# Order of weight loads, of the mixing's loads, and of transposes and fetches in the last gate of a two-layer Fox/RWKV and gMLP block

## The chip, the core and the metric

The kernel runs on one core of one Trainium2 chip. The metric is the device time of one execution in microseconds. The kernel before took 2281.07 us (median of three runs, 2279.98 to 2284.08).

## What is computed

A block of two layers on x (512 rows, 2048 columns), all in fp32. For each layer i:

```
h = h + rms_norm(y, norm_post[i])                       # y: the layer's own branch
h = h + (p[i] @ ple_w_proj[i]) * sigmoid(h @ ple_w_gate[i])
```

In layer 0, y comes from a forgetting attention and an RWKV time mix. In layer 1 it comes from a gated mixing of chunks of 128 rows:

```
u, v, g = split(rms_norm(h) @ c_w_in)                   # 3 x 2048 columns
v = layer_norm(gelu(v), c_ln_g, c_ln_b)
mixed[g] = tril(c_w_s[g]) @ v[chunk, group g] + c_b_s[g] # 16 groups of 128 columns
y = (gelu(u) * mixed * silu(g)) @ c_w_out
```

## The kernel before

TensorE (PE) gets fp32 accuracy by splitting each operand in a high and a low part, so that each product takes three matmuls. The weights' high part `whi` is a cast on ACT (L1387 in layer 1), the low part `wlo` a subtraction on DVE (L1388). There are four buffers of each, so these casts can run at most four pieces ahead of PE.

**The products of seven.** The products with `c_w_in` and with the last `ple_w_gate` are made by a scheme that needs seven block products instead of eight (`seven`, L1393 on). A *step* is one block product: eight *pieces* of W (128 x 512 each), with six matmuls per piece, so 48 matmuls. Layer 1's `c_w_in` takes 42 steps (called 0 to 41 below), the last gate in `last_layer` 14 more (42 to 55). I number the pieces of the last gate 0 to 111: step 42 is pieces 0 to 7, step 43 pieces 8 to 15, step 46 pieces 32 to 39, step 51 pieces 72 to 79.

**Where a piece of W comes from.** `pieces` (L1327) makes each pair of pieces from a tile of 128 x 1024. `load` brings it by a 512 KB DMA on SP's queue (L1338, tiles `raw` and `rq`). For some block products it is a sum of two blocks: `grow` adds the second block by an accumulating DMA on POOL's queue (L1342); `add` adds a tile that was loaded on its own (L1346, on DVE); and the product numbered 4 adds two 256 KB `half` tiles, loaded by SP (L1380, one buffer for each of two names), on DVE.

**What sets the order.** A tile scheduler puts each engine's instructions in order by priority and by when it expects their inputs. Each engine, SP and the DMA-issuing part of ACT included, then works strictly in that order: an instruction that waits holds up all behind it. The casts and the adds of W carry a raised priority (`wpri`, 150000 at this point); the loads of W do not. Side work is hung on a counter: `tick` counts pieces, and `later(n, step)` runs `step` n pieces on.

**The mixing.** `mix(g)` (L1491) is called for 16 groups during steps 21 to 27 and 35 to 41. Its four parts lie 11 and 4 pieces ahead of, at, and 5 pieces after a given piece: `load` brings the group's v (`vn<-vd`), `ws`, `ln_g` and `ln_b` by four DMAs on ACT's queue (L1502 to L1505), the last three into slices of one tile (`rstdB` or `accq`); `norm` normalises v with four ACT instructions (L1511) and multiplies and adds by the rows on DVE (L1515, L1516); `split` makes high and low parts (L1526, L1527); `mul` is the product (L1531 to L1533).

**The last gate.** `last_layer` (L1108) has side work in its 14 steps. `flip(g, m)` transposes a block of h on PE into one PSUM bank (four 128 x 128 matmuls, L1164), copies it out on ACT (L1166, into `xl`, or into the scratch tiles `sq` and `sg` for m = 2 and 3) and stores it to DRAM (`rd`, L1167). There are eight banks named `mm`, which the products share. `late(q)`, `s24(q)`, `s3(q)` and `x22` update h and make the other operands of the scheme, mostly on DVE. `fetch` loads the pieces of `pd` and `rd` that a result needs, 256 KB each, on SP (L1208, L1209), into tiles named `yh` at first and later into slices of two `xh` tiles that become free when `x22` has read them. `emit` makes the result (L1212 to L1215) and stores it (L1217).

The first layer's gate (`dense_all`, L970 on, with the loads and casts of L169 to L181) runs before layer 1: SP loads `raw` (L169), ACT and DVE split it (L179, L181), and the first loads of `c_w_in` for layer 1 are issued during it.

## Time and profile before

| | |
|---|---|
| median of three runs | 2281.07 us |
| profiled execution | 2283.18 us |
| its span on the core | 2281.5 us (1.7 us lie around it) |
| mean granted TensorE clock | 0.992 |
| instructions | 39072 |
| DMA traffic | 311.59 MB, mean 137 GB/s |
| first layer's gate | about 1190 to 1386 us |
| layer 1, steps 0 to 41 | up to 1874 us |
| last gate, steps 42 to 55 | 2086.15 to 2273.34 us |

The profiled execution lies 2.11 us (0.09%) above the median. A busy share is a mean over the whole span; the short waits in the stages that the change touches are read from the timelines and windows of those stages. A number in square brackets in a timeline is the time that the engine was idle just before, with what ended it.

### The profile page before, as it was taken

To read this page: it belongs to the slowest core of one execution; us is meant where nothing else is said; L and a number is where in the kernel's file an instruction comes from. 1 tells how busy PE (TensorE), PEld (TensorE's weight loads), DVE (VectorE), ACT (ScalarE), POOL (GpSimd) and SP (SyncE) were. 2 spreads that over 40 slices of the span, in tenths; PEclk is the share of its full clock that TensorE was granted. 3 is DMA by queue.
4 is the path that set the end of the run, shared out by engine and by line. 5 is a ranking of instruction groups with operands and counts; after the bars stand their busy time and mean duration, and the time that the engine had idled before them with its cause. 6 is when DMAs were issued, how large, how long until landed. Compare 5 with 4: busy or idle time off the path is not lost.

```text
span 2281.5 us, 39072 instructions
## 1 busy us (share of the span) xinstructions
PE 2228.9 (98%) x14787; PEld 1822.5 (80%) x14787; DVE 1476.4 (65%) x2885; ACT 1226.8 (54%) x2510; POOL 244.2 (11%) x302
## 2 busy tenths in 40 slices
PE   8999999999999999999999999999999999999988
PEld 7878888888887888878888888878778778887766
DVE  8666667666643878872237448778688684227867
ACT  5455555555443777753244547546566654335644
POOL 2000010010100000000010112101111110010020
PEclk9999999999999999999999999999999999999999
DMA  6322232223234533343335446776767774337696
GB/s 232 91 78 71 71 86 81 73 67 84 75 97 132 163 102 98 101 148 98 97 102 168 130 122 162 194 204 165 196 179 186 217 205 133 101 102 213 197 253 186
DMA packets 299482, 311.59 MB, mean 137 GB/s; under 512 B 15213, under 2 KB 198670, under 8 KB 298270
## 3 DMA queue, kind: packets, MB, share of 16 engines
q1 hardware_dynamic: 255390, 253.52, 36.6%
q0 software_dynamic: 17408, 33.56, 8.6%
q10 hardware_dynamic: 26496, 22.03, 3.1%
q8 instruction: 116, 1.90, 0.3%
q14 instruction: 72, 0.59, 0.1%
HBM read 274.15 MB, written 34.90 MB: 135 GB/s over the span
## 4 chain that ended last, share of the span: by engine, by line
PE 82%; DVE 7%; DMA 6%; ACT 3%; issue 2%; SPq 0%; ACTq 0%; DVEq 0%; POOLq 0%
PE mm L195 11%; PE mm L197 11%; PE mm L196 11%; PE mm L982 6%; PE mm L983 6%; PE mm L981 6%; PE mm L1415 6%; PE mm L1416 6%; PE mm L1417 6%; DVE wlo L1388 2%; PE tm L533 1%; DMA sq<-vd 1%; DVE rq L1346 1%; PE tm L554 1%; DMA rq<-in_ple_w_gate_dram 1%
## 5 line engine op out<-in xcount | busy, mean ns | idle before, releaser
L181 DVE TENSOR_TENSOR wlo<-raw,whi 128x512 fp32r<-128x512 f32 x464 | 331.6, 722 | 423.5 <-ACT whi L179 382.8
L179 ACT CAST whi<-raw 128x512 fp32r<-128x512 f32 x464 | 287.2, 620 | 459.0 <-PE mm L982 226.3
L196 PE MATMUL mm<-xl,whi 128*128 128x512 f32 x1088 | 427.2, 393 | 0.0
L195 PE MATMUL mm<-xh,whi 128*128 128x512 f32 x1008 | 418.2, 415 | 0.0
L197 PE MATMUL mm<-xh,wlo 128*128 128x512 f32 x1008 | 397.8, 395 | 0.0
L1387 ACT CAST whi<-rq 128x512 fp32r<-128x512 f32 x340 | 208.7, 620 | 161.2 <-PE mm L1417 89.9
L1388 DVE TENSOR_TENSOR wlo<-rq,whi 128x512 fp32r<-128x512 f32 x340 | 230.0, 687 | 86.3 <-ACT whi L1387 84.2
L196 PEld LDWEIGHTS mm<-xl,whi 128*128 128x128 f32 x1088 | 205.3, 189 | 33.4
L197 PEld LDWEIGHTS mm<-xh,wlo 128*128 128x128 f32 x1008 | 189.4, 188 | 41.7
L195 PEld LDWEIGHTS mm<-xh,whi 128*128 128x128 f32 x1008 | 190.0, 188 | 33.8
L981 PE MATMUL mm<-yl,whi 128*128 128x512 f32 x336 | 130.9, 390 | 0.0
L983 PE MATMUL mm<-yl,wlo 128*128 128x512 f32 x336 | 130.7, 389 | 0.0
L982 PE MATMUL mm<-xl,whi 128*128 128x512 f32 x288 | 112.0, 389 | 0.0
L1416 PE MATMUL mm<-wlo,yl 128*128 128x512 f32 x256 | 101.3, 396 | 9.1 <-DVE wlo L1388 9.1
L1459 POOL TENSOR_TENSOR accq<-accq,sq 128x512 f32<-128x512 f32 x42 | 56.8, 1352 | 478.6 <-ACT sq L1457 477.5
L1415 PE MATMUL mm<-whi,yh 128*128 128x512 f32 x256 | 101.3, 396 | 3.5 <-ACT whi L1387 3.5
L1415 PE MATMUL mm<-whi,xl 128*128 128x512 f32 x256 | 101.5, 396 | 2.5 <-ACT whi L1387 2.5
L1416 PE MATMUL mm<-wlo,yh 128*128 128x512 f32 x256 | 101.2, 395 | 1.4 <-DVE wlo L1388 1.3
L1416 PE MATMUL mm<-wlo,xl 128*128 128x512 f32 x256 | 100.9, 394 | 1.7 <-DVE wlo L1388 1.6
L1415 PE MATMUL mm<-whi,yl 128*128 128x512 f32 x256 | 101.3, 396 | 0.9 <-ACT whi L1387 0.9
L1417 PE MATMUL mm<-whi,yl 128*128 128x512 f32 x256 | 100.6, 393 | 0.0
L1417 PE MATMUL mm<-whi,yh 128*128 128x512 f32 x256 | 100.4, 392 | 0.0
(491 smaller groups left out, 4666.8 us busy)
## 6 DMA issues: line engine op xcount, KB each, us to landing
raw<-in_ab_w_in_dram SPq DMA_DIRECT2D x128, 512.0 KB, 4.0
rq<-in_c_w_in_dram SPq DMA_DIRECT2D x50, 512.0 KB, 5.8
raw<-in_ple_w_gate_dram SPq DMA_DIRECT2D x38, 512.0 KB, 4.1
rq<-in_c_w_in_dram POOLq DMA_DIRECT2D x36, 512.0 KB, 7.4
raw<-in_ab_w_out_dram SPq DMA_DIRECT2D x32, 512.0 KB, 3.7
raw<-in_c_w_out_dram SPq DMA_DIRECT2D x32, 512.0 KB, 3.8
raw<-in_c_w_in_dram SPq DMA_DIRECT2D x26, 512.0 KB, 3.7
rq<-in_ple_w_gate_dram SPq DMA_DIRECT2D x26, 512.0 KB, 3.7
```

The costliest lines, as they stand in the source:

```text
L179: nc.scalar.copy(hi[:, : m * n], src)
L181: self.weng.tensor_tensor(lo[:, : m * n], src, f(hi[:, : m * n]), ALU.subtract)
L195: nc.tensor.matmul(acc, hi, xhi[k], start=(k == 0), stop=False)
L196: nc.tensor.matmul(acc, hi, xlo[k], start=False, stop=False)
L197: nc.tensor.matmul(acc, lo, xhi[k], start=False, stop=(k == nk - 1))
L981: nc.tensor.matmul(accs[j], hi[:, js], xhi[k], start=(k == 0), stop=False)
L982: nc.tensor.matmul(accs[j], hi[:, js], xlo[k], start=False, stop=False)
L983: nc.tensor.matmul(accs[j], lo[:, js], xhi[k], start=False, stop=(k == nk - 1))
L1388: nc.vector.tensor_tensor(lo, src, f(hi), ALU.subtract)
L1415: nc.tensor.matmul(acc[m], xh, hi, start=(first and r == 0), stop=False, **more)
L1416: nc.tensor.matmul(acc[m], xh, lo, start=False, stop=False, **more)
L1417: nc.tensor.matmul(acc[m], xl, hi, start=False, stop=(r == 7), **more)
```

## The change

The change has four parts.

1. The 512 KB loads of W (L1338) and the `half` loads (L1380) get the raised priority `wpri`.
2. In the mixing, the loads of `ws`, `ln_g` and `ln_b` go from ACT's queue to SP's. The loads of v and `ws` are put inside `tc.issue_after(self.mm.ins)`, where `self.mm` is the last matmul issued.
3. In the last gate, the 16 flips are spread: ticks 1 to 8 become 6, 7, 9, 10, 12, 13, 15, 16, and ticks 30 to 37 become 29, 31, ... 43. `late(q)` goes from 2 + 4q to 1 + 4q, `s3(q)` from 38 + q to 36 + 2q, `x22` from 43 to 45.
4. The fetches of rows 2 and 3 for product 7 no longer run together at the end of a step; they follow 2 and 4 pieces into the next one. Those for product 4 are asked for at the same place.

```
-        steps = [(1 + k, lambda g=g, m=m: flip(g, m)) for k, (g, m) in enumerate(... for g in (2, 0, 3, 1) for m in (0, 1))]
-        steps += [(2 + 4 * q, lambda q=q: late(q)) for q in range(4)]
-        steps += [(16, early_spare)]
+        steps = flips(lambda k: 6 + 3 * k // 2, (0, 1)) + flips(lambda k: 29 + 2 * k, (2, 3))
+        steps += [(1 + 4 * q, lambda q=q: late(q)) for q in range(4)]
+        steps += [(16, early_spare), (45, x22), (47, late_spare)]
         steps += [(19 + 3 * q, lambda q=q: s24(q, less(q))) for q in range(4)]
-        steps += [(30 + k, lambda g=g, m=m: flip(g, m)) for k, (g, m) in enumerate(... for g in (2, 0, 3, 1) for m in (2, 3))]
-        steps += [(38 + q, lambda q=q: s3(q)) for q in range(4)]
-        steps += [(43, x22), (47, late_spare)]
+        steps += [(36 + 2 * q, lambda q=q: s3(q)) for q in range(4)]
...
                 elif prod == 7:
-                    fetch(pr.n + 1, (2, 3))
-                    if 4 in pr.done:
-                        fetch(pr.n, (2, 3))
-                elif prod == 4 and 7 in pr.done:
-                    fetch(pr.n, (2, 3))
+                    self.later(2, lambda: fetch(pr.n + 1, (2, 3)))
+                    self.later(4, lambda: fetch(pr.n, (2, 3)))
...
-            nc.sync.dma_start(view(tl), block(*where))
+            with self.tc.high_priority(self.wpri):
+                nc.sync.dma_start(view(tl), block(*where))
...
-                    nc.sync.dma_start(g, pr.W[k * P : (k + 1) * P, pr.c0 : pr.c0 + T])
+                    with self.tc.high_priority(self.wpri):
+                        nc.sync.dma_start(g, pr.W[k * P : (k + 1) * P, pr.c0 : pr.c0 + T])
...
-                nc.scalar.dma_start(vn, self.vd[:, g])
-                nc.scalar.dma_start(own["ws"], i["c_w_s"][0, g])
-                nc.scalar.dma_start(own["bc"][:, 0, :], i["c_ln_g"][0, gs].partition_broadcast(P))
-                nc.scalar.dma_start(own["bc"][:, 1, :], i["c_ln_b"][0, gs].partition_broadcast(P))
+                with tc.issue_after(self.mm.ins):
+                    nc.scalar.dma_start(vn, self.vd[:, g])
+                    nc.sync.dma_start(own["ws"], i["c_w_s"][0, g])
+                nc.sync.dma_start(own["bc"][:, 0, :], i["c_ln_g"][0, gs].partition_broadcast(P))
+                nc.sync.dma_start(own["bc"][:, 1, :], i["c_ln_b"][0, gs].partition_broadcast(P))
```

What this does to the order of the instructions, at the three places that the prediction speaks of:

**PE at the end of step 42.** These are PE's last rows of piece 7 and the first of piece 8 in the kernel before; L1164 are transposes of two flips, each of which needs a free PSUM bank.

```order
L1415 MATMUL mm_21837<-whi_21982,xh_4476_21620 128x512
L1416 MATMUL mm_21837<-wlo_21983,xh_4476_21620 128x512
L1417 MATMUL mm_21837<-whi_21982,xh_4477_21621 128x512
L1164 MATMUL mm_21974<-ident_114,yh_4343_20917 128x128 x2
L1164 MATMUL mm_21974<-ident_114,yh_4349_20933 128x128 x2
L1164 MATMUL mm_21998<-ident_114,yh_4343_20917 128x128 x2
L1164 MATMUL mm_21998<-ident_114,yh_4349_20933 128x128 x2
L1415 MATMUL mm_22009<-whi_22013,xh_4476_21620 128x512
```

In the changed kernel the same place reads as follows (the matmuls of `seven` are one line further down there); its flips stand behind pieces 5 (two), 8, 9, 12, 13, 14 and 17.

```order
L1418 MATMUL mm_21837<-whi_21942,xh_4477_21621 128x512
L1416 MATMUL mm_21961<-whi_21965,xh_4476_21620 128x512
L1417 MATMUL mm_21961<-wlo_21966,xh_4476_21620 128x512
L1418 MATMUL mm_21961<-whi_21965,xh_4477_21621 128x512
L1416 MATMUL mm_21962<-whi_21965,xh_4476_21620 128x512
L1417 MATMUL mm_21962<-wlo_21966,xh_4476_21620 128x512
L1418 MATMUL mm_21962<-whi_21965,xh_4477_21621 128x512
L1164 MATMUL mm_21975<-ident_114,yh_4287_20609 128x128 x2
L1164 MATMUL mm_21975<-ident_114,yh_4293_20625 128x128 x2
```

The two flips between the two steps are gone from that place. In the kernel before, their banks are those of the first two flips, whose copies stand on ACT behind the cast of piece 11, and the two banks of the new step are those of the third and fourth flip. In the changed kernel a flip that needs another flip's bank comes at piece 12 at the earliest, and its bank is copied out on ACT behind the casts of pieces 14, 15, 16 and 19.

**DVE and SP at the burst of fetches (steps 48 to 50).** On DVE, the last subtractions of `x22` (`yh<-xh`), which free the `xh` tiles for the fetches, stand like this before (`wlo_22722` to `wlo_22758` belong to pieces 54 to 56):

```order
L1388 TENSOR_TENSOR wlo_22722<-rq_4747_22630,whi_22721 128x512
L960 TENSOR_TENSOR yh_4733_22582<-xh_4404_21243,yh_4732_22581 128x512
L960 TENSOR_TENSOR yh_4726_22555<-sq_22552,yh_4725_22554 128x512
L1388 TENSOR_TENSOR wlo_22732<-rq_4747_22630,whi_22731 128x512
L1388 TENSOR_TENSOR wlo_22758<-raw_22011,whi_22757 128x512
L960 TENSOR_TENSOR yh_4735_22586<-xh_4404_21243,yh_4734_22585 128x512
L960 TENSOR_TENSOR yh_4737_22590<-xh_4435_21410,yh_4736_22589 128x512
```

and like this now (`wlo_22692` to `wlo_22712` belong to pieces 51 to 53):

```order
L1389 TENSOR_TENSOR wlo_22692<-rq_4727_22560,whi_22691 128x512
L960 TENSOR_TENSOR yh_4738_22605<-xh_4404_21243,yh_4737_22604 128x512
L960 TENSOR_TENSOR yh_4726_22557<-sq_22554,yh_4725_22556 128x512
L1389 TENSOR_TENSOR wlo_22702<-rq_4734_22591,whi_22701 128x512
L960 TENSOR_TENSOR yh_4740_22609<-xh_4404_21243,yh_4739_22608 128x512
L1389 TENSOR_TENSOR wlo_22712<-rq_4734_22591,whi_22711 128x512
L960 TENSOR_TENSOR yh_4742_22613<-xh_4435_21410,yh_4741_22612 128x512
L960 TENSOR_TENSOR yh_4744_22617<-xh_4435_21410,yh_4743_22616 128x512
```

The last of the four has moved from behind piece 57 to behind piece 53. SP's fetches and the loads of W behind them, before (`rq_4839` is a tile that step 51 adds on DVE):

```order
L1208 DMA xh_4750_22643<-pd_101 128x512 x3
L1209 DMA xh_4751_22644<-rd_102 128x512 x3
L1208 DMA xh_4750_22643<-pd_101 128x512
L1209 DMA xh_4751_22644<-rd_102 128x512
L1338 DMA raw_22971<-in_ple_w_gate_dram 128x2x512
L1208 DMA xh_4750_22643<-pd_101 128x512
L1338 DMA raw_22998<-in_ple_w_gate_dram 128x2x512
...
L1338 DMA rq_4826_23021<-in_ple_w_gate_dram 128x2x512
L1209 DMA xh_4751_22644<-rd_102 128x512 x2
L1338 DMA rq_4831_23044<-in_ple_w_gate_dram 128x2x512
L1338 DMA rq_4839_23072<-in_ple_w_gate_dram 128x2x512
```

and now:

```order
L1210 DMA xh_4750_22643<-pd_101 128x512 x3
L1211 DMA xh_4751_22644<-rd_102 128x512 x3
L1210 DMA xh_4750_22643<-pd_101 128x512
L1338 DMA raw_22971<-in_ple_w_gate_dram 128x2x512
L1211 DMA xh_4751_22644<-rd_102 128x512
L1338 DMA raw_22998<-in_ple_w_gate_dram 128x2x512
...
L1338 DMA rq_4826_23021<-in_ple_w_gate_dram 128x2x512
L1219 DMA out_dram<-xh_4751_22644 128x512
L1338 DMA rq_4831_23044<-in_ple_w_gate_dram 128x2x512
L1211 DMA xh_4751_22644<-rd_102 128x512
L1338 DMA rq_4839_23072<-in_ple_w_gate_dram 128x2x512
```

Of twelve fetches that stood ahead of `rq_4839`, ten are left, and the two fetches from `rd` that stood together ahead of `rq_4831` no longer do.

**SP in the first layer's gate.** Before (`raw` are this gate's own weights, `rq` and `half` those of layer 1):

```order
L169 DMA raw_14295<-in_ple_w_gate_dram 128x2x512
L1338 DMA rq_3219_15774<-in_c_w_in_dram 128x2x512
L169 DMA raw_14341<-in_ple_w_gate_dram 128x2x512
L1338 DMA rq_3224_15796<-in_c_w_in_dram 128x2x512
L1338 DMA rq_3234_15833<-in_c_w_in_dram 128x2x512
L1338 DMA rq_3239_15855<-in_c_w_in_dram 128x2x512
L169 DMA raw_14387<-in_ple_w_gate_dram 128x2x512
```

and now:

```order
L169 DMA raw_14295<-in_ple_w_gate_dram 128x2x512
L1338 DMA rq_3219_15774<-in_c_w_in_dram 128x2x512
L1338 DMA rq_3224_15796<-in_c_w_in_dram 128x2x512
L1338 DMA rq_3234_15833<-in_c_w_in_dram 128x2x512
L1338 DMA rq_3239_15855<-in_c_w_in_dram 128x2x512
L1338 DMA rq_3244_15877<-in_c_w_in_dram 128x2x512
L1338 DMA rq_3249_15899<-in_c_w_in_dram 128x2x512
L1381 DMA half_3358_16393<-in_c_w_in_dram 128x512
L1381 DMA half_3359_16396<-in_c_w_in_dram 128x512
L169 DMA raw_14341<-in_ple_w_gate_dram 128x2x512
L169 DMA raw_14387<-in_ple_w_gate_dram 128x2x512
L1505 DMA rstdB_12776<-in_c_w_s_dram 128x128
```

The gate's next tile, `raw_14341`, has moved behind six 512 KB and two 256 KB loads for layer 1.

**ACT in the mixing.** The order of every engine is the same with and without `issue_after`, which orders only instructions of one engine, while `self.mm` is PE's and the loads are ACT's and SP's. With the three other loads gone from ACT's queue, the first instruction of `norm` stands nearer behind its v load: in four of the 16 groups, where 9, 6, 7 and 6 other instructions lay between them, 2, 2, 2 and 3 do now. On SP, 48 loads of 64 KB now stand among the loads of W.

More of the change, by code (lines that the diff above doesn't have):

```diff
@@ L1190, in x22 @@
             sets[4] = self.set22(H, wp, False)
-        steps = [(1 + k, lambda g=g, m=m: flip(g, m)) for k, (g, m) in enumerate((g, m) for g in (2, 0, 3, 1) for m in (0, 1))]
-        steps += [(2 + 4 * q, lambda q=q: late(q)) for q in range(4)]
-        steps += [(16, early_spare)]
+        flips = lambda at, ms: [
+            (at(k), lambda g=g, m=m: flip(g, m))
+            for k, (g, m) in enumerate((g, m) for g in (2, 0, 3, 1) for m in ms)
+        ]
+        steps = flips(lambda k: 6 + 3 * k // 2, (0, 1)) + flips(lambda k: 29 + 2 * k, (2, 3))
+        steps += [(1 + 4 * q, lambda q=q: late(q)) for q in range(4)]
+        steps += [(16, early_spare), (45, x22), (47, late_spare)]
         steps += [(19 + 3 * q, lambda q=q: s24(q, less(q))) for q in range(4)]
-        steps += [(30 + k, lambda g=g, m=m: flip(g, m)) for k, (g, m) in enumerate((g, m) for g in (2, 0, 3, 1) for m in (2, 3))]
-        steps += [(38 + q, lambda q=q: s3(q)) for q in range(4)]
-        steps += [(43, x22), (47, late_spare)]
+        steps += [(36 + 2 * q, lambda q=q: s3(q)) for q in range(4)]
         for n, step in steps:
@@ L1416, in seven @@
                             nc.tensor.matmul(acc[m], xh, lo, start=False, stop=False, **more)
-                            nc.tensor.matmul(acc[m], xl, hi, start=False, stop=(r == 7), **more)
+                            self.mm = nc.tensor.matmul(acc[m], xl, hi, start=False, stop=(r == 7), **more)
                     rows = []
```

## Prediction

> **What bounds the kernel now.** I read the page first: its engine line, to see who is short of time.
>
> ```profile
> span 2281.5 us, 39072 instructions
> PE 2228.9 (98%) x14787; PEld 1822.5 (80%) x14787; DVE 1476.4 (65%) x2885; ACT 1226.8 (54%) x2510; POOL 244.2 (11%) x302
> ```
>
> PE is busy for 98% of the span. The change removes no matmul, so all it can win is the 2281.5 - 2228.9 = 52.6 us in which PE is idle, and matmuls that run slowly at a low granted clock. Next I cut the last gate into its steps with the windows view (columns: window, length, busy time of PE, PEld, DVE, ACT, POOL, granted clock, DMA share, GB/s). Steps 42 to 44 and 46 to 53:
>
> ```profile
> 2086.15:2104.54 18.39, 15.14 (x82) 11.95 (x80) 17.45 (x30) 13.11 (x25) 2.41 (x2) 0.97 0.96 292
> 2104.54:2118.28 13.74, 13.74 (x48) 11.08 (x49) 6.14 (x10) 7.47 (x14) 2.41 (x2) 0.79 0.97 263
> 2118.28:2129.16 10.88, 10.88 (x49) 9.01 (x48) 9.80 (x16) 8.17 (x15) 0.00 (x0) 1.00 0.96 292
> ...
> 2141.33:2160.00 18.67, 14.76 (x71) 11.64 (x70) 18.06 (x28) 12.16 (x21) 0.00 (x0) 0.95 0.23 77
> 2160.00:2171.74 11.74, 11.74 (x50) 9.65 (x49) 7.82 (x13) 6.19 (x11) 0.00 (x0) 0.93 0.76 255
> 2171.74:2182.62 10.88, 10.88 (x49) 9.01 (x48) 10.88 (x19) 8.37 (x16) 4.55 (x4) 1.00 0.90 166
> 2182.62:2194.39 11.77, 11.18 (x50) 8.94 (x48) 10.05 (x18) 5.84 (x10) 0.26 (x1) 1.00 1.04 308
> 2194.39:2205.68 11.29, 11.05 (x50) 8.83 (x48) 5.01 (x9) 3.80 (x7) 3.61 (x3) 1.00 1.07 282
> 2205.68:2225.81 20.13, 13.42 (x49) 10.23 (x50) 12.26 (x17) 6.37 (x11) 4.83 (x4) 0.83 1.04 258
> 2225.81:2238.91 13.10, 11.50 (x50) 8.85 (x48) 9.86 (x17) 5.19 (x9) 1.21 (x1) 1.00 0.88 204
> 2238.91:2251.43 12.52, 12.00 (x50) 8.70 (x49) 11.34 (x20) 6.59 (x13) 0.00 (x0) 1.00 0.77 245
> ```
>
> Step 44 is an undisturbed step: 10.88 us, all PE, clock 1.00. That is 1.36 us per piece. Three places lose time against it: the turn from step 42 to 43, the end of step 46, and steps 49 to 53, with step 51 the worst. PE's timeline says why:
>
> ```profile
> 2102.51 1.14 PE L1164 MATMUL mm<-ident,yh 128*128 128x128 f32 x8 [2.37 <-ACT xl L1166]
> 2104.54 0.79 PE L1415 MATMUL mm<-whi,xh 128*128 128x512 f32 x1 [0.88 <-ACT xl L1166]
> ...
> 2154.66 0.66 PE L1164 MATMUL mm<-ident,xh 128*128 128x128 f32 x4 [1.68 <-ACT sq L1166]
> 2157.22 0.66 PE L1164 MATMUL mm<-ident,xh 128*128 128x128 f32 x4 [1.90 <-ACT sg L1166]
> ...
> 2216.16 0.80 PE L1416 MATMUL mm<-wlo,yl 128*128 128x512 f32 x1 [5.79 <-DVE wlo L1388]
> ```
>
> The first two places wait for flips to be copied out of PSUM, the third for a weight.
>
> **The change, part by part.** I work on the profiled execution, 2283.18 us, and subtract its 2.11 us above the median at the end.
>
> *Flips of the first half (steps 42, 43).* The copy that PE waits for stands on ACT behind the cast of piece 11, which needs the buffer that PE gives back only at the end of piece 7:
>
> ```profile
> 2100.82 0.63 ACT L1387 CAST whi<-raw 128x512 fp32r<-128x512 f32 x1
> ...
> 2101.86 1.08 ACT L1166 COPY xl<-mm 128x512 f32<-128x512 f32 x2
> ```
>
> So PE must stand still for cast, cast and copy. In the changed order nothing at the turn needs a flip's bank. The first such flip follows piece 12 and needs a copy behind the cast of piece 14, whose buffer came free after piece 10: two pieces, 2.72 us, for a cast and a copy of about 0.6 us each. Those waits should go. PE's work in step 42 is 15.14 us with all eight flips in it; step 43's is 10.88 us at full clock. So 18.39 + 13.74 - 15.14 - 10.88 = 6.1 us can be won at most; 3.25 of it are waits and 2.86 step 43's low clock (0.79). DVE limits this: 17.45 us busy out of 18.39 in step 42. The new order puts the eight flips' 4.3 us (15.14 - 10.88) mostly into step 43 and so asks for step 42's pieces sooner, but it also moves two of the 30 DVE instructions past them. I take -5.5, with -3 and -6.1 as ends.
>
> By the Trainium skill (page "TensorE: Matmul & The Clock Gate", section "What's actually happening") the clock falls only after an idle window of about 3.4 us. The trace differs: 2.37 and 0.88 us of idling with 1.14 us of transposes between them were enough. By the page's figure alone, a split wait such as this would not be followed by a slow clock, and the term would be the waits alone, -3.25.
>
> *Flips of the second half (step 46).* The three waits there end on copies that stand behind the cast of piece 43 in both orders, behind the end of step 46 itself. Two flips stay at that place, two go behind pieces 40 and 42, where they wait for results that DVE writes later; and the two banks of step 47 now need the third and fourth flips' copies. The windows give a loss of 18.67 - 14.76 = 3.9 us of waits and 11.74 - 10.88 = 0.9 of low clock. I take 0, ends -2.5 (half of it goes) and +2.5 (the two moved flips wait as long as the 1.68 us row, and slow clock).
>
> *Fetches, `x22` and the loads behind them (steps 48 to 53).* DVE waits for a loaded tile, and so does PE; the chain of waits goes back to its load at 2200.15, and SP's queue shows what stood ahead:
>
> ```profile
> 2214.28 1.23 DVE L1346 TENSOR_TENSOR raw<-raw,rq 128x1024 f32<-128x1024 f32 x1 [7.33 <-DMA rq<-in_ple_w_gate_dram]
> ```
>
> ```profile
> 2200.15 12.17 DMA rq<-in_ple_w_gate_dram
> ```
>
> ```profile
> 2182.40 1.36 SPq L1208 DMA_DIRECT2D xh<-pd  x3
> ...
> 2195.34 0.50 SPq L1338 DMA_DIRECT2D rq<-in_ple_w_gate_dram  x1
> 2198.48 1.57 SPq L1209 DMA_DIRECT2D xh<-rd  x2
> 2200.15 3.44 SPq L1338 DMA_DIRECT2D rq<-in_ple_w_gate_dram  x5
> ```
>
> The fetches start when `x22` has read the `xh` tiles. Its last subtraction moves four pieces ahead, 4 x 1.36 = 5.4 us. Two of twelve 256 KB fetches move behind the tile that is waited for: 0.52 MB at the 282 GB/s of step 50 is 1.9 us. Together 7.3 us, against a DVE wait of 7.33 us and 6.71 us of PE idling in step 51 (20.13 - 13.42). If the wait goes, so does the low clock behind it (13.42 - 10.88 = 2.5 us). Steps 49, 50, 52 and 53 lost 0.9, 0.4, 2.2 and 1.6 us more. All five lost 14.4 us. Not all of this comes back, since the DMA engines have no slack: their share is 1.04 to 1.07 in steps 49 to 51. I take -7; the ends are -2 (only the fetches' order counts) and -12 (nearly all).
>
> *The mixing's loads on SP.* What ACT wins is the issuing of three loads in each of 16 groups:
>
> ```profile
> 1685.51 0.34 ACTq L1503 DMA_DIRECT2D accq<-in_c_w_s_dram  x1
> 1685.89 0.45 ACTq L1504 DMA_DIRECT2D accq<-in_c_ln_g_dram  x1
> 1686.46 0.36 ACTq L1505 DMA_DIRECT2D accq<-in_c_ln_b_dram  x1
> ```
>
> That is 1.15 us x 16 = 18 us on an engine that is busy for 54% of the span, so about nothing on the path. What it costs is on two engines. On ACT, `norm` comes closer behind its v load, and six groups wait for that load already:
>
> ```profile
> ACT sq L1511 <- DMA sq<-vd: 20.0, 6, 5.6
> ```
>
> ```profile
> 1686.92 0.65 PE L1415 MATMUL mm<-whi,xl 128*128 128x512 f32 x1 [2.49 <-ACT whi L1387]
> ```
>
> The casts are queued behind `norm`. Of the longest wait, 5.6 us, 2.49 reached PE, so about 3.1 us are covered by the cast pieces. The mean wait is 20.0 / 6 = 3.3 us, and four more groups can now wait as much: 0.2 us each if at the mean, 2.5 if at the longest. On SP, a row's load waits for its buffer, and the `half` loads for the next step, with one buffer each, stand behind it:
>
> ```profile
> 1669.87 0.68 DVE L1515 TENSOR_TENSOR sq<-sq,rstdB 128x512 f32<-128x512 f32 x1
> ```
>
> ```profile
> 1668.63 5.70 SPq L1380 DMA_DIRECT2D half<-in_c_w_in_dram  x4
> ```
>
> The `ln_g` load needs the end of that multiplication, 1670.55, and one `half` load issued at 1668.63 now stands behind it: 1.9 us late. I take +2 in sum, ends -2 (ACT's shorter queue spares one of the waits) and +8 (two to three waits of the longest kind, with clock). `issue_after` I cost at nothing, since it moves no instruction.
>
> *Priority of W's loads in the first layer's gate.* 3.67 MB (six tiles of 0.52 and two of 0.26) now precede `raw_14341` on SP:
>
> ```profile
> 1212.68 0.37 SPq L1338 DMA_DIRECT2D rq<-in_c_w_in_dram  x1
> ```
>
> ```profile
> 1221.00:1230.00 9.00, 9.00 (x41) 7.44 (x41) 8.74 (x15) 4.42 (x9) 0.00 (x0) 1.00 1.03 374
> ```
>
> ```profile
> 1221.10 0.62 ACT L179 CAST whi<-raw 128x512 fp32r<-128x512 f32 x1
> ...
> 1223.35 0.62 ACT L179 CAST whi<-raw 128x512 fp32r<-128x512 f32 x1 [1.11 <-PE mm L982]
> ```
>
> At the 374 GB/s of the second row, 4.19 MB with the tile itself take 11.2 us from 1212.68 on, so it lands about 1224 to 1227 instead of before its cast at 1221.10. Casts run ahead until PE gives a buffer back (the 1.11 us wait), which is three more pieces of 12 matmuls, some 8 us. That covers a delay of 5 us. I take +0.5; ends 0 and +3, if DVE's updates (8.74 of 9.00 us busy) also come between.
>
> Sum: -5.5 + 0 - 7 + 2 + 0.5 = -10. The profiled execution would take 2273.2, the median 2271.1 us.
>
> **The rivals.**
>
> *The DMA engines stay the bound in steps 49 to 53.* For it: the shares of 1.04 to 1.07, and who uses them (DMA view from 2160 to 2230: packets, MB, share of 16 engines):
>
> ```profile
> q0 software_dynamic: 2998, 5.78, 47.5%
> q1 hardware_dynamic: 5434, 10.14, 44.2%
> ```
>
> Almost half of the DMA time there is POOL's accumulating loads, which no order on SP overtakes. Then an earlier burst only meets those, and step 51 still waits. Against it: the rate was 166 GB/s in step 48, at a share of 0.90, but 308 in step 49, at 1.04, so more could be moved beside them. Then -2 stands for -7, and the time is 2276. The Trainium skill (page "DMA: Bandwidth & Descriptors", section "Queues, rings and completion order") says that each DMA engine goes round-robin between the queues that have work; by that rule SP's precedence holds on its own queue alone, and the trace's 47.5 and 44.2% agree with an even split.
>
> *Slower: the mixing pays for its loads.* Four more groups wait like the longest, on ACT, with the casts behind: 2.5 us on PE and, as after the turn of step 42, up to 2.9 of low clock, so 4 x 5.4 = 22 us. With the rest of the sum (-5.5 - 7 + 0.5) the time is 2283.2 - 12 + 22 - 2.1 = 2291. It decides from waits of about 3.1 us on. Against it: four of these groups had 6 to 9 instructions between, and the six that waited already had 2 to 9; a mean of 3.3 us is just at the bound.
>
> *The stalls of the flips only move.* DVE can't bring step 42's weights in time, and PE waits for `wlo` instead. Then -5.5 becomes -1, and the time 2275.6.
>
> *The change does not do what it says* is true of one part: the v load isn't tied to its row, since the order is the same without the tie. Had it held the load back, the six waits would be longer; it is in the sum at nothing.
>
> **How the numbers follow.** A measurement of this kernel can tell about 0.2%, 4.6 us: faster is below 2276.5, slower above 2285.6. Forecast (a gain from 5 to 19 us) 0.65; DMA bound at 2276, half of it faster, 0.13; flips only move, 0.08, a little more than half faster; mixing pays, 0.10 (a third of it only back to 2281); two smaller costs at their ends together, 0.04. Faster 0.65 + 0.065 + 0.045 = 0.76; slower 0.08; the rest, 0.16, within. The range goes from the sum with the better ends of the two large terms, 2283.2 - 6.1 - 12 - 2 - 2.1 = 2261, to the case where DMA bound and mixing's +8 meet, 2283.2 - 5.5 - 2 + 8 - 2.1 = 2281.6; I take 2261 to 2281.
>
> **What would show it.** Right: no wait on ACT `xl` L1166 at the turn of step 42, and steps 42 and 43 together in 26 to 28 us; step 46 still near 18 us; DVE's wait for `rq` in step 51 under 2 us; ACT's waits for v more than six. Wrong: step 51 still at 20 us; a PE wait for `wlo` in step 42; more than 15 us of PE idling in steps 21 to 41; PE idle near 1229.

## The result and the profile after

The changed kernel takes 2292.18 us (median of 6 runs, 2289.01 to 2295.89), the kernel before on the same chip 2279.28: ratio 1.0054, 95% interval 1.004 to 1.0069. It is slower by about 12 us, where 10 us of gain were forecast. A second measurement (in the last experiment) gave 1.0040 (1.0025 to 1.0054). The profiled execution took 2291.12 us.

The page of the changed kernel, its engine line:

```profile
span 2289.4 us, 39090 instructions
PE 2233.1 (98%) x14787; PEld 1820.3 (80%) x14787; DVE 1477.0 (65%) x2885; ACT 1225.2 (54%) x2510; POOL 243.0 (11%) x302
```

PE is idle for 56.3 us now (52.6 before), and its matmuls show 4.2 us more. The windows view cuts the last gate into steps (columns as in the prediction). First steps 42 to 47 and 48 to 53 whole, then steps 42, 43, 45, 46, 47 and 51:

```profile
2092.67:2180.75 88.08, 79.54 (x353) 64.01 (x352) 74.75 (x119) 56.13 (x100) 4.81 (x4) 0.92 0.70 217
2180.75:2258.90 78.15, 69.75 (x290) 54.45 (x288) 56.50 (x88) 34.93 (x61) 14.47 (x12) 0.98 0.96 249
2092.67:2104.45 11.78, 11.78 (x58) 9.84 (x56) 11.78 (x21) 7.28 (x13) 1.17 (x1) 1.00 0.88 286
2104.45:2117.84 13.39, 13.39 (x70) 10.90 (x69) 12.56 (x21) 11.24 (x21) 3.64 (x4) 1.00 1.10 278
...
2129.26:2147.34 18.08, 15.05 (x57) 11.72 (x56) 11.64 (x20) 10.57 (x18) 0.00 (x0) 0.81 0.64 216
2147.34:2166.46 19.12, 13.61 (x65) 10.55 (x64) 18.43 (x28) 10.72 (x20) 0.00 (x0) 0.95 0.26 84
2166.46:2180.75 14.29, 14.29 (x56) 11.68 (x57) 11.36 (x19) 8.55 (x16) 0.00 (x0) 0.82 0.57 200
...
2213.39:2231.99 18.60, 13.68 (x50) 9.87 (x49) 11.14 (x16) 5.70 (x10) 3.63 (x3) 0.91 1.08 267
```

The same two long stretches before, and step 45 before:

```profile
2086.15:2171.74 85.59, 78.43 (x353) 63.43 (x352) 71.40 (x113) 55.53 (x97) 4.81 (x4) 0.94 0.73 223
2171.74:2251.42 79.68, 70.01 (x289) 54.56 (x288) 59.38 (x95) 36.15 (x64) 14.46 (x12) 0.96 0.96 245
2129.16:2141.33 12.17, 12.17 (x61) 10.10 (x60) 12.13 (x20) 8.42 (x15) 0.00 (x0) 1.00 0.65 206
```

Steps 42 and 43 fell from 32.13 to 25.17 us, as forecast. Steps 45 to 47 rose from 42.58 to 51.49. Steps 48 to 53 stayed: 79.68 and 78.15, with the DMA engines at a share of 0.96 in both. In step 45, PE waits for two casts, and they stand behind work that waits for a store: first PE's timeline of the changed kernel, then ACT's and DVE's.

```profile
2136.81 0.50 PE L1416 MATMUL mm<-whi,yl 128*128 128x512 f32 x1 [1.95 <-ACT whi L1388]
2138.39 0.79 PE L1417 MATMUL mm<-wlo,yl 128*128 128x512 f32 x1 [1.08 <-DVE wlo L1389]
```

```profile
2135.62 0.62 ACT L959 CAST xl<-sq 128x512 fp32r<-128x512 f32 x1 [4.24 <-DMA rd<-xl]
...
2137.05 0.69 DVE L960 TENSOR_TENSOR xl<-sq,xl 128x512 fp32r<-128x512 f32 x1 [4.70 <-DMA rd<-xl]
```

`s24` writes its result into a tile `xl` from which a flip's store to `rd` still reads. It is one of the flips of the first half. Before, ACT copied it out behind the cast of piece 16, with eleven casts of W between that copy and this cast. Now the copy stands behind the cast of piece 24, with three casts between.

The other loss lies in steps 21 to 41, from 463.1 to 471.5 us. Such lengths run from the start of step 21 to the start of step 42. They take in the product with `c_w_out`, which lies between step 41 (in the kernel before it ends at 1884.8 us, not at 1874) and step 42. That product took 201.3 us in every profiled run, so what differs is the steps. The view of waits from 1610 to 1895 us (engine, what it waited for: total, times, longest), after:

```profile
ACT sq L1513 <- DMA sq<-vd: 34.9, 10, 5.4
...
PE mm L1416 <- ACT whi L1388: 6.1, 7, 1.7
```

and before, where ACT's own row is the one in the prediction:

```profile
PE mm L1415 <- ACT whi L1387: 2.5, 1, 2.5
```

ACT waits for v ten times instead of six, as forecast, and seven such waits come through to PE instead of one.

How far do such numbers hold? A profiled run is one execution. I therefore give the lengths of the stretches, from PE's timelines, as means over all profiled runs with the same order there: for the last gate, eight runs with the order of before and seven with that of the change; for steps 21 to 41, seven and six.

| us | order of before (lowest to highest) | of the change | difference | forecast |
|---|---|---|---|---|
| steps 21 to 41 | 464.4 (462.8 to 466.7) | 472.5 (471.3 to 473.7) | +8.1 | +2 |
| steps 42, 43 | 31.1 (29.3 to 32.2) | 25.2 (25.1 to 25.2) | -5.9 | -5.5 |
| step 44 | 10.9 | 11.4 | +0.5 | |
| step 45 | 12.2 (12.2 to 12.5) | 15.0 (12.9 to 18.1) | +2.8 | |
| steps 46, 47 | 31.0 (30.0 to 32.2) | 33.9 (33.0 to 34.8) | +2.9 | 0 |
| steps 48 to 53 | 78.3 (75.9 to 80.7) | 78.5 (78.0 to 79.2) | +0.2 | -7 |

The sum is +8.6 us, a ratio of 1.0038. It fits the second measurement (1.0040); the first lies higher, with its interval from 1.004 on.

### The profile page after: what moved, and what is told of

It reads as the page before. It is cut to its first block, busy times and chain, and to the rows that moved or that the text cites. A ratio compares the mean times of both kernels' runs of the same rounds, so it can differ in the third digit from the quotient of the medians.

```text
span 2289.4 us, 39090 instructions
## 1 busy us (share of the span) xinstructions
PE 2233.1 (98%) x14787; PEld 1820.3 (80%) x14787; DVE 1477.0 (65%) x2885; ACT 1225.2 (54%) x2510; POOL 243.0 (11%) x302
## 5 line engine op out<-in xcount | busy, mean ns | idle before, releaser
L1416 PE MATMUL mm<-whi,yh 128*128 128x512 f32 x256 | 101.6, 397 | 5.2 <-ACT whi L1388 5.2
L1416 PE MATMUL mm<-whi,xl 128*128 128x512 f32 x256 | 101.9, 398 | 3.1 <-ACT whi L1388 2.0
L1418 PE MATMUL mm<-whi,xl 128*128 128x512 f32 x256 | 100.5, 393 | 0.0
```

The lines of the kernel that those rows point to most:

```text
L1416: nc.tensor.matmul(acc[m], xh, hi, start=(first and r == 0), stop=False, **more)
L1418: self.mm = nc.tensor.matmul(acc[m], xl, hi, start=False, stop=(r == 7), **more)
```

## Experiments

Each ratio is to the kernel before on the same chip, with its 95% interval.

### The parts one by one

The last gate alone (the diff's third and fourth part):

> The kernel before with the change's last gate only (flips, late, s3, x22 and the fetches spread; no priority for loads of W, the mixing's loads on ACT as before). Theory A (each part keeps its own effect, as read from the step table of the changed kernel): steps 42 and 43 together 7 us shorter than before, steps 45 to 47 about 9 us longer because casts of s24 wait for stores of flips, steps 48 to 53 about 1.5 us shorter: within 2 us of the kernel before in all. Rival B (the stall in step 45 comes from SP's new order of the loads of W, which delays the flips' stores in the DMA engines): steps 45 to 47 as before, and 7 to 9 us faster in all.

Measured: 0.9993 (0.9978 to 1.0008). Steps 42 and 43 took 25.16 us, 45 to 47 48.13, 48 to 53 78.43. The gain is made and given back on the spot, without the other parts.

The priority alone (`high_priority` around the loads at L1338 and L1380):

> The kernel before with the raised priority for the loads of W only. Theory A: the 1.5 us that the changed kernel was ahead at the start of layer 1 and the 1.2 us of step 11 come from this part: 1 to 3 us faster, nothing else moves by over 1 us. Rival B (the priority also delays v's loads in the mixing by putting loads of W ahead of them): steps 21 to 41 are 2 us or more longer than before.

Measured: 0.9997 (0.9985 to 1.0009). It costs nothing that can be told.

`ws`, `ln_g` and `ln_b` on SP's queue alone:

```
-                nc.scalar.dma_start(own["ws"], ...)      # and both ln loads
+                nc.sync.dma_start(own["ws"], ...)
```

> The kernel before with the mixing's loads of ws, ln_g and ln_b on SP only. Theory A (the norm stands nearer behind its v load on ACT, so more norms wait and the casts queued behind them reach PE): steps 21 to 41 are 5 to 8 us longer, ACT waits for v 9 to 11 times instead of 6; 5 to 8 us slower in all. Rival B (the mixing's loss needs the priority as well): within 2 us of before.

Measured: 1.0024 (1.0012 to 1.0037), steps 21 to 41 in 471.33 us. And the changed kernel with these three loads back on ACT:

> The changed kernel with the mixing's three other loads back on ACT's queue (so: priority for W's loads, and the changed last gate). Theory A (the move to SP is what costs most): the 8 us that steps 22 to 41 lose in the changed kernel and in the move alone come back, ACT waits for v six or seven times; 6 to 10 us faster than the changed kernel, within 4 us of before. Rival B (the priority and the new last gate together lose more than the sum of each alone): still 6 us or more slower than before.

Measured: 1.0006 (0.9994 to 1.0017), steps 21 to 41 in 463.78 us. The mixing's loads are the part that makes the change slow.

The changed kernel without `issue_after`:

> The changed kernel without issue_after. Its instructions stand in the same order on every engine. Theory A (the tie does nothing, as predicted): the same time as the changed kernel, 10 to 13 us slower than before, and step by step the same trace but for chance. Rival B (the tie holds something back on the chip): 3 us or more faster than the changed kernel.

Measured: 1.0058 (1.0042 to 1.0074) against 1.0054 with it. The tie does nothing that can be told.

### Why the mixing costs

The same three loads on POOL's queue (`nc.gpsimd.dma_start`), with SP's order as before:

> The kernel before with the mixing's loads of ws, ln_g and ln_b on POOL's queue instead of ACT's: ACT's order is that of the move to SP (norm two instructions behind its v load), SP's order is that of before. Theory A (the loss comes from ACT's order, norms that wait for v with casts behind them): steps 22 to 41 lose 5 to 9 us as with the move to SP, ACT waits for v 9 to 11 times. Rival B (the loss comes from SP, where row loads hold up loads of W): within 2 us of before, whatever ACT waits.

Measured: 1.0057 (1.004 to 1.0074), steps 21 to 41 in 478.93 us. The waits in these steps:

```profile
ACT sq L1511 <- DMA sq<-vd: 41.0, 10, 7.3
...
PE mm L1415 <- ACT whi L1387: 11.1, 7, 4.1
```

SP's queue is untouched here, and the loss is still there, larger. So it isn't SP's `half` loads that are held up; DVE's waits for `half` in this stretch sum to 3.1 us with the loads on SP and 3.0 us with them on POOL, against 4.3 us before. What both runs share is that ACT no longer issues the three loads between the load of v and the norm. Why POOL costs 7 us more than SP isn't shown.

Then I tied the norm's ACT instructions behind the last cast of W that the program makes before them, first on the kernel with the loads on SP, then on the kernel before:

```
+                with tc.issue_after(self.cast.ins):      # self.cast: the last cast of W
                     for m in range(4):
                         nc.scalar.activation(vn[:, m, :], ...)
```

> The mixing's loads on SP, alone on the kernel before, with norm's four ACT instructions tied by issue_after to the last cast of W on ACT at their tick. In the order, 4 to 8 casts then stand between v load and norm in eight of the groups that had 2, still 1 or 2 in the others. Theory A: ACT waits for v fall from 34 us to under 20, and steps 22 to 41 are 3 to 7 us shorter than with the move alone. Rival B (SP): the loss of the move stays, within 2 us of it.

> The kernel before with one edit: in the mixing, the norm's instructions on ScalarE may not be placed ahead of the last cast of the piece of W that stands before them in the program; the loads of ws and ln stay on ScalarE's queue, and the last gate is as before. Theory (the price is ScalarE waiting for v behind a load that it issued two instructions earlier, while casts of W stand behind the wait): ScalarE's waits for v fall below 20 us in sum and steps 22 to 41 get shorter by 0 to 6 us, ratio 0.9975 to 1.0. Rival (the place of ws and ln in a queue is what costs, and the norm's place does not matter): nothing changes against before, waits at 20 us or more, ratio 0.9995 to 1.0005. If the norm comes so late that sg is late for its matmuls, waits of TensorE for sg appear in steps 22 to 41 and the time is up to 5 us longer, ratio up to 1.002.

Measured: 1.0008 (0.9995 to 1.0022) and 1.0033 (1.0021 to 1.0045). In the first, ACT's waits for v fall from 34.2 to 19.3 us, PE's waits for `whi` from 5.5 us to none, and steps 21 to 41 come back from 471.3 to 465.3 us, though PE now waits 11.4 us for the mixing's own operand `sg` (3.4 without the tie):

```profile
ACT sq L1512 <- DMA sq<-vd: 19.3, 9, 4.1
```

With the loads on POOL, this makes the norm's place behind v's load the cost. The waits of the second:

```profile
ACT sq L1512 <- DMA sq<-vd: 11.2, 4, 3.9
PE mm L1534 <- DVE sg L1528: 11.1, 5, 3.5
PE mm L1533 <- ACT sg L1527: 1.5, 1, 1.5
```

ACT's waits for v fall to 11.2 us, but now the mixing's own matmuls wait for `sg`: 12.6 us, against 3.8 before. The norm can stand too late as well as too early. On the first kernel the same move paid (1.0024 to 1.0008), though the intervals overlap; on the second it cost.

### The last gate: store, buffers or DMA

The changed kernel with `s24` four pieces later, so that its cast comes after the store has landed:

```
-        steps += [(19 + 3 * q, lambda q=q: s24(q, less(q))) for q in range(4)]
+        steps += [(23 + 3 * q, lambda q=q: s24(q, less(q))) for q in range(4)]
```

> The changed kernel with s24 four pieces later (ticks 23 to 32 instead of 19 to 28). Theory A (in step 45 ACT and DVE stand still because the second s24 writes xl tiles whose stores to DRAM by the flips, now later, are still under way): the 4.2 us wait of the cast on rd<-xl goes, step 45 takes 11 to 13 us instead of 18.1, 5 to 9 us faster than the changed kernel. Rival B (DVE has too much to do in steps 45 to 47 whatever the stores do): step 45 shortens but steps 46 and 47 grow by as much, within 2 us of the changed kernel.

Measured: 1.0023 (1.001 to 1.0037). The wait for the store is gone, and step 45 takes 12.51 us, as before the change: it was the store that step 45 paid for. Steps 46 and 47 stay at 33.92 us and 48 to 53 at 78.81.

The kernel before with only its first flips moved (at 5 + k, `late` at 1 + 4q, `s24` at 21 + 3q), and a version that joins this with the norm's tie, the priority and the spread fetches:

> The kernel before with only the flips of the last gate's first half moved: the first four one piece apart, at pieces 5 to 8, the late four at 1, 5, 9 and 13, and the second sum's piece s24 two pieces later than before (at 21, 24+...: every third from 21), so that its cast into xl stands six pieces behind the store that it waits for, not two. Second half, fetches and loads as before. Theory (the gain of the flips is real, and step 45 gave it back because the cast into xl stands too close behind the flip's store): steps 42 and 43 together 25 us (32.13 before), step 45 at 12 to 13 (18.09 in the changed kernel, 12.17 before), the time 4 to 6 us shorter, ratio 0.9975 to 0.998. Rival (the stalls only move: the accumulators and buffers of the first half are short whatever the order): 45 to 47 longer by 4 or more again, ratio 0.9995 to 1.0005.

> The first flips' edit (flips at 5 to 8 and 1, 5, 9, 13, s24 from 21 on), the tie of the norm to the last cast of W, the priority for W's loads and the spread fetches of the last steps, without ws and ln on SyncE's queue. If both theories hold (step 45 pays for the cast's place, the mixing for the wait on v) the gains add: 5 to 6 us from steps 42 and 43, 0 to 6 from steps 22 to 41, 0 to 2 from steps 49 to 53: 6 to 13 us shorter than before, ratio 0.994 to 0.9975. If the stalls only move, ratio 0.999 to 1.001.

Measured: 1.0015 (1.0002 to 1.0029) and 1.0019 (1.0006 to 1.0033). My hope for them failed. Steps 42 and 43 took 25.6 us in both, but step 45 took 16.71 and 17.37. In the first, ACT waits there for a piece of W:

```profile
2129.06 0.62 ACT L1387 CAST whi<-rq 128x512 fp32r<-128x512 f32 x1 [4.55 <-DMA rq<-in_ple_w_gate_dram]
```

The store is out of the way, and now a load is late. That pointed to the DMA engines. So I cut their traffic and moved nothing: the accumulating loads of the last gate bring 16 of 128 rows, in the kernel before and in the one with only the last gate changed. Both kernels leave out 7/8 of the second block in the pieces that are sums, so their result is not that of the block. (Of the two weights that `pieces` loads, only the last gate's has 2048 columns.)

```
-            nc.gpsimd.dma_start(view(tl), block(*where), accum_op=ALU.add)
+            nc.gpsimd.dma_start(*(x[: 16 if pr.W.shape[-1] == 2048 else P] for x in (view(tl), block(*where))), accum_op=ALU.add)
```

> The kernel before, with the accumulating loads on GpSimd's queue in the last gate cut to 16 of their 128 rows; no instruction of any other engine moves. It leaves out 7/8 of the second block in the pieces of W that are sums. Theory (from step 48 to 53 the DMA engines are the bound, so no order of flips, fetches or x22 changes that stretch): steps 48 to 53 fall from 78.2 us (mean of the six profiled runs with the order of before, 75.9 to 80.7) to 66 to 70, the time by 8 to 12 us, ratio 0.995 to 0.9965. Rival (DVE's subtractions of x22 and the tiles they free set that stretch): steps 48 to 53 stay at 76 or more, ratio 0.999 to 1.001.

> The changed kernel's last gate alone on the kernel before (as in the run with only the last gate's part), with the same cut of the accumulating loads; it leaves out the same part. Theory (what the flips won in steps 42 and 43 is given back in step 45 because loads and stores are not landed yet on busy DMA engines): steps 42 and 43 in 25.2 us, step 45 at 12 to 13, steps 46 and 47 at 31 to 32, the last gate 4 to 6 us shorter than in the kernel before with the same cut. If the giving back sits in DVE or in the accumulators: step 45 at 14 or more, or steps 46 and 47 at 33 or more, and the last gate within 2 us of the kernel before with the same cut.

Measured: 0.9934 (0.9915 to 0.9954) and 0.992 (0.9896 to 0.9944). The windows of steps 48 to 53 whole and of step 51, in the kernel before with the cut:

```profile
2164.30:2234.41 70.11, 66.98 (x289) 53.52 (x288) 59.13 (x94) 36.06 (x63) 9.51 (x12) 1.00 0.67 198
...
2196.93:2210.07 13.14, 11.46 (x50) 8.78 (x49) 10.23 (x14) 5.33 (x9) 3.17 (x4) 1.00 0.54 167
```

and with the new order and the cut, steps 45 and 46 between them:

```profile
2163.84:2229.29 65.45, 65.45 (x289) 53.97 (x288) 56.41 (x88) 35.74 (x61) 9.51 (x12) 1.00 0.71 215
...
2118.76:2130.98 12.22, 12.14 (x58) 9.71 (x56) 10.25 (x18) 9.94 (x17) 0.00 (x0) 1.00 0.70 229
2130.98:2150.34 19.36, 13.79 (x66) 10.74 (x64) 19.07 (x29) 10.61 (x20) 0.00 (x0) 0.91 0.30 99
...
2196.48:2207.36 10.88, 10.88 (x50) 9.01 (x48) 10.88 (x17) 5.50 (x9) 3.17 (x4) 1.00 0.29 67
```

With less traffic, steps 48 to 53 fall from 78.3 to 70.1 us, and the new order of flips and fetches takes them down to 65.45: six times 10.88 is 65.3, so nothing is lost any more. Step 45 is at 12.22 us, under the 12.87 to 18.08 us of the seven runs with the same order and full traffic, and ACT's wait for the store there is 1.28 us, under their 1.69 to 4.25. The last gate takes 169.1 us against 175.7, and 185.3 in the mean of the eight runs with the old order and full traffic. (The ratio of the cut kernel before stands for 15 us, its last gate for 9.6; the rest isn't explained, it lies ahead of step 21, where the order is that of before.) So the DMA engines were the bound in steps 48 to 53, and busy DMA engines made step 45 slow; each of the two cut kernels was profiled once. Steps 46 and 47 don't follow: 32.86 us with the new order, 29.75 with the old one. PE's timeline of step 46 there:

```profile
2144.68 0.66 PE L1164 MATMUL mm<-ident,xh 128*128 128x128 f32 x4 [1.68 <-ACT sq L1166]
2148.84 1.11 PE L1164 MATMUL mm<-ident,xh 128*128 128x128 f32 x4 [3.50 <-ACT sg L1166]
```

The copy for which PE waits 3.5 us stands on ACT behind the fourth sum's two casts (L959), which wait for DVE:

```profile
2146.22 0.62 ACT L959 CAST xl<-sq 128x512 fp32r<-128x512 f32 x1 [1.59 <-DVE sq L1278]
2147.68 0.62 ACT L959 CAST xl<-sg 128x512 fp32r<-128x512 f32 x1 [0.84 <-DVE sg L1281]
2148.20 0.58 ACT L1166 COPY sg<-mm 128x512 f32<-128x512 f32 x1
```

That wait was 1.90 us in the kernel before. In the changed kernel and the six other runs with its order it is 2.7 to 3.5 us, and step 47 begins with another wait of 0.7 to 1.4 us for a copy of the same kind. With `s24` four pieces later, step 46 has no wait, and step 47 waits 2.32 us for one copy and 3.69 us for another that stands behind the same two casts; these wait 4.14 and 0.62 us for DVE. So the casts of the fourth sum hold up that copy. DVE is busy for 19.07 of the 19.36 us above, so it may be DVE that sets this step; that part wasn't tried by itself.

### v on SP's queue

If v's load is too close ahead of the norm on ACT, it might be issued elsewhere. The kernel before with v alone on SP:

```
-                nc.scalar.dma_start(vn, self.vd[:, g])
+                nc.sync.dma_start(vn, self.vd[:, g])
```

> The kernel before with only the mixing's load of v on SyncE's queue; ws and ln stay on ScalarE's. TensorE's order is that of before. Theory (the price of the mixing is ScalarE reaching the norm while v, loaded on its own queue two instructions earlier, is still on its way): v is issued ahead of ScalarE's place, its waits for v fall below 15 us, and steps 21 to 41 get 0 to 5 us shorter, ratio 0.998 to 1.0005. Rival (a load on SyncE's queue that waits for a buffer holds up the loads of W behind it): waits for rq, raw or half by ScalarE and DVE grow, steps 21 to 41 are 3 to 15 us longer, ratio 1.001 to 1.006.

Measured: 0.9964 (0.9948 to 0.998), 2275.93 us: faster than both kernels. But the gain isn't where I looked for it. Steps 21 to 41 take 464.17 us, as before, and ACT's waits for v are 27.6 us. Most of it lies in steps 11 and 12, of which the windows of the kernel before show:

```profile
1508.34:1523.25 14.91, 11.39 (x50) 8.93 (x49) 8.80 (x16) 5.12 (x10) 4.81 (x4) 1.00 0.94 198
1523.25:1536.04 12.79, 12.79 (x49) 10.14 (x50) 9.57 (x17) 7.06 (x12) 0.00 (x0) 0.87 0.92 281
```

and with v on SP:

```profile
1505.06:1515.94 10.88, 10.88 (x50) 9.01 (x48) 9.86 (x17) 6.02 (x11) 4.81 (x4) 1.00 0.89 183
1515.94:1526.82 10.88, 10.88 (x50) 9.01 (x48) 7.88 (x15) 6.16 (x10) 0.00 (x0) 1.00 1.11 303
```

ACT's timeline of the kernel before gives the cause. The first load of v waits on ACT until a store of v has landed, and a cast of W stands behind it:

```profile
1522.14 0.34 ACTq L1502 DMA_DIRECT2D sq<-vd  x1
1522.58 0.62 ACT L1387 CAST whi<-rq 128x512 fp32r<-128x512 f32 x1 [7.25 <-DMA vd<-comb]
```

PE loses 3.52 us there, then the clock of step 12 is 0.87: together 27.70 - 21.76 = 5.9 us. The ratio stands for 8 us, with an interval from 5 to 12, so the rest can't be told from chance. The two steps took 24.8 to 30.7 us in every run with v on ACT, the changed kernel among them (13.71 + 13.16 = 26.9), and neither the change nor my prediction saw it.

To see whether this holds, I put v on SP in the changed kernel, once with `ws` and `ln` back on ACT and once with all four loads on SP:

> The changed kernel with ws and ln back on ScalarE's queue and v on SyncE's queue in their place: the priority for W's loads and the new last gate stay. Theory (v's load on ScalarE's queue costs 6 us in steps 11 and 12, where it waits for v's store with a cast of W behind it; the last gate's new order is worth nothing because the DMA engines bound it): steps 11 and 12 in 21.8 us together, the last gate within 3 us of 184.7, the time 6 to 9 us shorter than before, ratio 0.996 to 0.9975. Rival (the gain of the run with v on SyncE alone came with its chip and its day, ahead of step 21 where layer 0 varies): ratio 0.999 to 1.001.

> The changed kernel with v on SyncE's queue too, so that all four loads of a group of the mixing are issued there. Theory (a group costs only what ScalarE waits for v beyond the 3.1 us that its lead in cast pieces covers): steps 11 and 12 fall to 21.8 us, and steps 21 to 41 follow the waits for v: about 463 to 466 us if the waits beyond 3.1 us add up to less than 5 us, about 471 or more if they add up to 8 or more; time 2 to 7 us shorter than the changed kernel, ratio to before 1.002 to 1.0045. Rival (loads on SyncE's queue that wait for a buffer hold up W): waits for rq, raw or half grow and steps 21 to 41 are longer than the changed kernel's 471.5.

Measured: 0.9978 (0.9968 to 0.9988) and 1.0016 (1.0002 to 1.0031). Steps 11 and 12 took 21.8 us in both. Steps 21 to 41 took 468.7 and 478.2 us. By my rule of waits beyond 3.1 us (8.3 us in sum in the second) some 471 were expected there; that rule alone doesn't carry. What does is how much of ACT's lateness comes through to PE. One profiled run for each row, the norm untied; the column "beyond 3.1 us each" is summed from the single waits:

| ws, ln / v issued by | ACT's waits for v, us | beyond 3.1 us each | PE's waits for `whi`, us | steps 21 to 41, us |
|---|---|---|---|---|
| ACT / ACT (priority alone) | 20.0 | 2.2 | 1.2 | 462.8 |
| ACT / ACT (kernel before) | 20.0 | 2.8 | 2.5 | 463.1 |
| ACT / SP | 27.6 | 3.1 | 1.4 | 464.2 |
| ACT / ACT (last gate alone) | 23.2 | 5.1 | 3.5 | 466.4 |
| ACT / SP (with the change) | 32.3 | 7.2 | 4.6 | 468.7 |
| SP / ACT (alone) | 34.2 | 8.7 | 5.5 | 471.3 |
| SP / ACT (changed kernel) | 34.9 | 8.4 | 6.1 | 471.5 |
| SP / SP (with the change) | 37.9 | 8.3 | 10.0 | 478.2 |
| POOL / ACT | 41.0 | 15.0 | 11.1 | 478.9 |

From the first row to the last, each us that PE waits for `whi` goes with (478.9 - 462.8) / (11.1 - 1.2) = 1.6 us of time. That the loads of W are late instead isn't seen: with all four loads on SP, DVE's waits for `half` are 3.1 us and ACT's 0.7 us.

### Do the parts add up?

The priority and the mixing's loads together, with the old last gate; and the changed kernel again on the same chip:

> The changed kernel with the last gate of before: the priority for W's loads and ws and ln on SyncE's queue, without the tie. Each part alone gave 0.9993 (last gate), 0.9997 (priority) and 1.0024 (mixing), together 1.0014, where the whole change measured 1.0054. If the priority and the mixing's loads meet on SyncE's queue and cost more together than apart: ratio 1.004 to 1.0055, steps 21 to 41 at 474 us or more. If it is the last gate that is dearer in the whole change than alone: ratio 1.002 to 1.003, steps 21 to 41 at 471 to 473 us. If the surplus came with the chip of that measurement: 1.002 to 1.003 here and the repeat of the changed kernel at 1.002 to 1.004 too.

> The changed kernel once more, beside the run with its priority and its mixing loads alone, on the same chip. If the parts add up as they stand, the ratio is 1.001 to 1.003; if the first measurement holds, 1.004 to 1.0065; the step table gives 1.0037 (5.6 us won in steps 42 and 43, 5.9 lost in 44 to 47, 0.3 in 48 to 53 and 7.8 in 21 to 41, 8.4 us in sum).

Measured: 1.0031 (1.0016 to 1.0047) and 1.0040 (1.0025 to 1.0054), with steps 21 to 41 in 473.1 and 472.8 us. The parts alone add up to 1.0014, with an uncertainty of 0.0012 to 0.0015 on each; these two runs lie between that and the first 1.0054. An extra cost of the parts together isn't shown.

## Why the prediction was wrong

**Flips of the first half: right in steps 42 and 43, wrong behind them.** -5.5 was forecast, -5.9 measured; the wait for `xl` L1166 is gone, PE doesn't wait for `wlo` in step 42, and both steps take 25.2 us, a little under the 26 to 28 named. (0.5 us of it has only moved: one flip now stands in step 44.) The low clock that was counted in it varies by chance: with the same wait at the turn, step 43 of the old order took 11.02 to 13.91 us in eight runs, at a granted clock of 1.00 in the shortest of these and 0.79 in the kernel before. So idling of 2.37 and 0.88 us wasn't always enough for a low clock, and no run here tells whether the 1.14 us of transposes between them count as idling too. But a flip that moves later also issues its store later, and the sum `s24` needs the tile that this store reads. The prediction followed the banks of a flip and not its store, and so put steps 44 and 45 at nothing: that step failed. Step 45 pays 0.7 to 5.9 us, 2.8 in the mean; ACT's wait for the store in these runs is 1.69 to 4.25 us.

**Flips of the second half: 0 taken, +2.9 measured in steps 46 and 47.** The prediction named the two banks of step 47 that now need a flip's copy, and the two moved flips that wait for DVE, and took 0 all the same, with +2.5 as the worse end. Step 46 grew by 0.6 us, step 47 by 2.3: its first matmul waits 1.15 us for such a copy in the changed kernel, and the granted clock is 0.82 there (0.93 before). That flips' copies stand behind casts of the fourth sum, which wait for DVE, is shown; why DVE is late for these casts stays open. All flips together come to -5.9 + 0.5 + 2.8 + 2.9 = +0.3. So the rival that their stalls only move was near in number, though not by its mechanism, a wait for `wlo` in step 42.

**Fetches: wrong, +0.2 in place of -7.** The step that failed is the overlap, "more could be moved beside them", taken from step 49's 308 GB/s. Steps 48 to 53 stayed at a DMA share of 0.96. The first rival, that the DMA engines stay the bound, was right, and was given 0.13; it allowed even 2 us too much. The mechanism itself was real: with the traffic cut, the same order brought 70.1 down to 65.45 us, 4.7 us. DVE's wait in step 51 shows the failure in the changed kernel, 3.09 us where under 2 was named (with only the last gate changed it was 8.44, against 7.33 before):

```profile
2217.12 1.23 DVE L1346 TENSOR_TENSOR raw<-raw,rq 128x1024 f32<-128x1024 f32 x1 [3.09 <-DMA rq<-in_ple_w_gate_dram]
```

By the Trainium skill (page "DMA: Bandwidth & Descriptors", section "Queues, rings and completion order") each DMA engine takes its queues in turn. The cut of POOL's loads, which changed no order on SP and brought steps 48 to 53 from 78.3 to 70.1 us, agrees, as it would with any sharing of the engines.

**The mixing: right mechanism, wrong size.** Ten waits for v in place of six were forecast and came, with the casts behind them. +2 was taken and +8.1 measured, the named end. The mean of the new waits, 3.5 us, is near the 3.3 assumed; but they reach from 0.3 to 5.4 us, and what lies beyond the 3.1 us that are covered adds up to 8.4 us, against 2.8 before. Pricing the four added waits at the mean, just at the bound, hid that: this is the term that was mis-sized. And I priced PE's waits alone. Of the 8.4 us by which the profiled steps 21 to 41 grew, 4.6 are PE's idling (9.8 to 14.4 us) and 3.8 are PE's busy time (251.9 to 255.8 us); the sign named for this case, more than 15 us of idling, was just missed. The rival with 22 us was too dear: PE's longest wait for `whi` there was 1.7 us, and the granted clock stayed at 1.00 in steps 24 to 29. That its time, 2291, lies close to the measured 2292 is luck: it kept the gain of the fetches, which didn't come, and priced the mixing at nearly three times what it cost.

**Tie and priority: right.** The tie was put at nothing and the priority at +0.5 us; neither can be told from nothing, and PE doesn't idle near 1229.

The sum by the same steps is -5.9 + 0.5 + 5.7 + 0.2 + 8.1 = +8.6 where -10 stood: 7 us from the fetches, 6 from the work behind the flips, 6 from the mixing. The errors all had one sign: each term was counted at the place of its wait, without asking what else the moved instruction releases and what is next late there.

## What to carry to other kernels

Where the DMA engines' share is near 1, as in steps 48 to 53 here, ask first whether a better order of loads can gain anything: here it gained nothing until the traffic was cut. When an instruction moves, follow everything that it issues, and the tile that it reads, to the next writer of that tile. And a load's issue is itself an instruction in an engine's line: what it waits for holds up the casts behind it, and what stands between it and its user is the lead that the load has.

## What was not expected of the hardware

Loads from POOL's queue are dear. In the kernel before, steps 48 to 53, the DMA view shows (packets, MB, share of 16 engines):

```profile
q1 hardware_dynamic: 7068, 13.17, 50.1%
q0 software_dynamic: 3264, 6.29, 45.2%
```

POOL's accumulating loads take 45.2 / 6.29 = 7.2% per MB, the others 50.1 / 13.17 = 3.8%. Each accumulated MB held the engines about 1.9 times as long. How much of this is the accumulating and how much the queue isn't shown. The queue alone has a price: the mixing's three loads, which add nothing up, brought POOL's queue in steps 21 to 41 alone (without `c_w_out`) from 28.2% of 261.7 us to 34.3% of 277.6 us. The same view, before and with the loads on POOL:

```profile
q0 software_dynamic: 6528, 12.58, 28.2%
q0 software_dynamic: 7744, 15.08, 34.3%
```

The difference is 21 us of the 16 engines' time for 2.5 MB. On ACT's queue the same loads took 12 us (its share was 11.3% of 261.7 us with them, 6.4% of 277.6 us without).

Which engine issues a load mattered by more than the time of the issue. The Trainium skill (page "DMA: Bandwidth & Descriptors", section "Issuing engines are not separate DMA queues") says that issuing from several engines only saves time on the sequencer. Here the same loads made steps 21 to 41 take 464 us from ACT, 472 from SP and 479 from POOL, and v's load from SP spared 5.9 us in steps 11 and 12. The transfers may share the engines, but a wait sits in the line of whoever issues: a cast stood 7.25 us behind v's load on ACT.
